# Fourteen block products for the output projection, and mixer A's gates moved behind its queries, keys and values

## The chip, the cores and the metric

The kernel runs on one core of one Trainium2 chip. A core has TensorE (matmuls, written to PSUM), VectorE, ScalarE, GpSimd, SyncE, whose queue issues most of the DMAs, and 16 DMA engines. In the profile they are PE (PEld for its weight loads), DVE, ACT, POOL and SP. The metric is the device time of one execution in microseconds.

## The reference

One encoder layer on 512 tokens of width 2048, with 16 meta tokens put in front (528 positions). All is float32.

```
hn   = rmsnorm(h, pre_norm_g)
proj = hn @ w_in                                  # 2048 -> 6656 columns
qa, ka, va, ga, qb, kb, vb, gb = split(proj)
ya = gqa_axial(qa, ka, va) * silu(ga)             # 8 heads of 128, 2 key/value heads, axial rotary
yb = diff_attn_alibi(qb, kb, vb) * silu(gb)       # 8 heads, each softmax1 - lam * softmax2, then a norm
y  = concat(ya, yb) @ w_out                       # 2048 x 2048
out = (h + rmsnorm(y, post_norm_g))[meta tokens dropped]
```

Mixer A norms queries and keys per head (RMS, times a gain), turns them by a rotary angle of the token's row and column, and attends. Mixer B subtracts two softmaxes with a distance penalty and norms the result per head.

## The kernel before

Every float32 product is done with three matmuls on float32r parts: an operand is split in a high part (`hi`, ScalarE, L325; for weights L158) and a low part (`lo`, VectorE, L328; for weights L159), and high x high, low x high and high x low are added in PSUM. So each dense column block of 128 over 16 slices of the inner dimension takes 48 matmuls of 512 columns (`REAL`), or 96 of 264 when the meta tokens are needed too (`KEYS`). All matmuls come from one line (`mm`, L63), all transposes from another (`transpose`, L66).

The order of TensorE is written by hand. `Lanes` (L45) has a planner's clock: each matmul adds its cost (512 columns 0.216 us by that clock, 264 columns 0.111), and each attention step is a generator that yields the lag after which its next step is due (the table `LAG`, L32). While a dense block runs, `lanes.poll()` after every three matmuls lets due steps in. `finish_head` runs a head's steps to their end at once (`force`), jumping the clock ahead to each due time, with no dense matmuls between. Everything so recorded stays in that order on TensorE (`keep_in_program_order`). The other engines' order is chosen by the framework's scheduler, apart from the loads through `load` (L143), which keep theirs too.

Weights come in chunks of 512 KB through `fetch`, which keeps two chunks ahead of the one in use; staging tiles, high parts and low parts have three buffers each. `wsplit` splits a chunk under a priority `rank[0]`.

Stages: loads of x and the first blocks; mixer B's heads (for each head a value, a key, a query and a gate block, with the attention of the head before beside them); mixer A's blocks in the order key 0, value 0, key 1, value 1, queries of group 0, two gates, queries of group 1, six gates (`GATES`); then the output. A head of mixer B has scores, softmax, a transposition of p through the PSUM tiles of the tag "tr" (two buffers), p times v, and `finish_B` with its norm matmul "ss" and the product with the gate. A head of mixer A multiplies p times v with its gate on VectorE (L585). Heads are written to DRAM (`oscr`).

The output (L827 on) takes 512 columns at a time. Groups 0 and 3 are computed whole (`dense_out`): 16 slices, 4 row tiles, 3 matmuls. The last four heads run beside group 0. Groups 1 and 2 are computed together from seven block products of 256 rows x 1024 inner x 512 columns (`product`), which need sums of blocks of w_out and sums of halves of the heads. The sums of weights are made in DRAM during mixer B, by a copy on SP's queue and an accumulating DMA on GpSimd's (`weigh`, 16 of each). At the end each row tile is scaled by its norm, added to the residual and written (`row_block`, L1028).

Of the kernel before, what the change touches and what calls it, by code (L numbers as in the profile page):

```python
# [10 lines left out]
F32 = mybir.dt.float32  # L11
# [24 lines left out]
LATE = ()  # L36
# [7 lines left out]
class Lanes:  # L44
# [13 lines left out]
    def mm(self, out, lhsT, rhs, start, stop):  # L58
# [4 lines left out]
        self._add(self.nc.tensor.matmul(out, lhsT, rhs, start=start, stop=stop), us)  # L63
# [45 lines left out]
def kernel(ctx: ExitStack, tc: tile.TileContext, xT, xn, xm, w_s, w_t, w_q, w_o,  # L109
# [8 lines left out]
    wp = ctx.enter_context(tc.tile_pool(name="wp", bufs=3))  # L118
    dr = ctx.enter_context(tc.tile_pool(name="dr", bufs=1, space=DRAM))
# [55 lines left out]
    for i in range(16):  # L175
# [3 lines left out]
    xh, xl = [[xp.tile([P, 576], F32R, name=f"x{n}{k}", tag=f"x{n}{k}")[:, :NT]  # L179
               for k in range(KT)] for n in "hl"]  # L180
# [77 lines left out]
    for t in (TT, 0, 1, 2, 3):  # L258
        rows = P if t < TT else NM
        src = xn[t * P:(t + 1) * P, :] if t < TT else xm  # L260
        for j in range(2 if t < 2 else 4):
# [4 lines left out]
            st = ap.tile([P, w], F32, name="xns", tag=tag, bufs=2 if t < 2 else 4)[:rows]  # L266
# [28 lines left out]
    cosT = ctile([P, TT, P], "cosT", src=cos_d, pool=ap)  # L295
    sinT = ctile([P, TT, P], "sinT", src=sin_d, pool=ap)
# [74 lines left out]
    def values(pss):  # L371
# [8 lines left out]
        def turn():  # L380
            tr = ptr.tile([P, 512], F32, name="tr", tag="tr")
# [5 lines left out]
            yield LAG["bank"]  # L387
            tr = ptr.tile([P, 512], F32, name="tr", tag="tr")
# [7 lines left out]
    def gate(pss, name):  # L396
        g = ap.tile([P, SEQ], F32, name=name, tag="g", bufs=4)
# [5 lines left out]
    pv_last, p_live = [None], [0]  # L403

# [14 lines left out]
    def p_times_v(pts, v, done, gate_of):  # L419
# [28 lines left out]
        while gate_of is not None and len(gA) <= gate_of:  # L448
            yield 0.3
        pv = ptr.tile([P, 512], F32, name="pv", tag="tr")  # L450
# [7 lines left out]
        mm(o, vm, pm, start=False, stop=True)  # L458
        done(o)
# [48 lines left out]
    def finish_B(h, o):  # L508
        while gB[h] is None and h not in LATE:
            yield 1.0  # L510
# [15 lines left out]
        if h in LATE:  # L526
            gB[h] = ap.tile([P, SEQ], F32, name=f"gB{h}", tag="g", bufs=4)
            nc.scalar.activation(gB[h], o, AF.Copy, scale=sgc)
        else:
            nc.vector.scalar_tensor_tensor(out=gB[h], in0=o, scalar=sgc, in1=gB[h],  # L530
                                           op0=ALU.mult, op1=ALU.mult)
# [171 lines left out]

# [429 lines left out]
```

## Time and profile before

| | us |
|---|---|
| median of 3 runs | 925.81 |
| lowest and highest | 925.52, 925.96 |
| the profiled execution | 925.19 |
| its span, first to last instruction | 923.4 |
| granted TensorE clock, share | 0.998 |

The span is what the trace covers; 1.8 us of the profiled execution lie around it. Busy times of engines overlap, so they don't add up to the span. Matmuls are pipelined and their ends are modelled: a matmul of 512 columns is shown as 0.39 us though the next one starts after about 0.23, so the pace is read from starts, or from a long unbroken stretch of the chain. A group "xN" has N instructions; the mean is of one of them.

### The profile page before, as it was taken

How to read it: one execution, taken by the hardware profiler on the slowest of the kernel's cores; microseconds unless marked ns; L12 is line 12 of the kernel's file. 1: busy time of each engine (PE TensorE's matmuls, PEld its weight loads, DVE VectorE, ACT ScalarE, POOL GpSimd, SP SyncE). 2: the span in 40 equal slices, each digit the busy share in tenths (PEclk: the TensorE clock that was granted, in tenths of full speed). 3: DMA queues.
4: the chain of work that ended last, by engine and by line, in shares of the span. 5: the costliest groups of instructions: out<-in, count | busy, mean ns of one | idle time of the engine just before them, and what ended most of it. 6: DMA issues, size and time to landing. Idle time of an engine off the chain costs nothing.

```text
span 923.4 us, 14263 instructions
## 1 busy us (share of the span) xinstructions
PE 911.5 (99%) x5498; PEld 807.2 (87%) x5498; DVE 576.7 (62%) x1029; ACT 486.5 (53%) x849; POOL 120.4 (13%) x164
## 2 busy tenths in 40 slices
PE   9999999999999999999999999999999999999995
PEld 8999898998989899898999888888888888888884
DVE  6676575847567575665766247447645574654797
ACT  6564564638455474654754254437555662524661
POOL 0102010111101010010010020115111111200110
PEclk9999999999999999999999999999999999999999
DMA  9845533644536364231223223221222162775884
GB/s 342 284 140 144 152 108 111 159 128 144 142 109 178 92 169 139 70 104 69 85 67 102 92 84 98 70 80 58 81 74 76 57 217 91 263 221 166 296 308 183
DMA packets 43892, 128.11 MB, mean 139 GB/s; under 512 B 5104, under 2 KB 9072, under 8 KB 43568
## 3 DMA queue, kind: packets, MB, share of 16 engines
q1 hardware_dynamic: 40416, 115.66, 37.1%
q0 software_dynamic: 3264, 11.54, 6.7%
q8 instruction: 43, 0.70, 0.3%
q14 instruction: 25, 0.20, 0.1%
q10 hardware_dynamic: 144, 0.01, 0.0%
HBM read 118.80 MB, written 25.17 MB: 156 GB/s over the span
## 4 chain that ended last, share of the span: by engine, by line
PE 93%; DVE 4%; ACT 1%; issue 1%; POOL 0%; DMA 0%; DVEq 0%; ACTq 0%; POOLq 0%
PE pd L63 60%; PE po L63 16%; PE sc L63 7%; PE pv L63 5%; PE tr L66 5%; DVE y L1028 1%; DVE wl L159 1%; PE ss L63 0%; DMA gcol<-in_gpre_dram 0%; DVE l L328 0%; DVE y L1040 0%; DVE qn L605 0%; POOL ssh L247 0%; DVE y L1034 0%; ACT jk L602 0%
## 5 line engine op out<-in xcount | busy, mean ns | idle before, releaser
L63 PE MATMUL pd<-xh,wh 128*128 128x264 f32 (+1 forms) x992 | 331.8, 334 | 0.2 <-ACT wh L158 0.2
L63 PE MATMUL pd<-xl,wh 128*128 128x264 f32 (+1 forms) x992 | 323.0, 326 | 0.0
L63 PE MATMUL pd<-xh,wl 128*128 128x264 f32 (+1 forms) x992 | 322.7, 325 | 0.1
L158 ACT ACTIVATE wh<-st 128x1024 fp32r<-128x1024 f32 (+2 forms) x147 | 152.8, 1040 | 210.3 <-issue 88.0
L159 DVE TENSOR_TENSOR wl<-st,wh 128x1024 fp32r<-128x1024 f32 (+2 forms) x147 | 176.4, 1201 | 113.7 <-ACT wh L158 112.6
L63 PEld LDWEIGHTS pd<-xh,wl 128*128 128x128 f32 x992 | 186.4, 188 | 16.3 <-DVE wl L159 0.3
L63 PEld LDWEIGHTS pd<-xh,wh 128*128 128x128 f32 x992 | 186.7, 188 | 11.7 <-ACT wh L158 0.4
L63 PEld LDWEIGHTS pd<-xl,wh 128*128 128x128 f32 x992 | 187.1, 189 | 10.6 <-DVE xl L187 0.4
L490 ACT ACTIVATE p<-p,mx 128x528 f32<-128x528 f32 x64 | 47.0, 734 | 43.2 <-DVE mx L482 42.9
L63 PE MATMUL po<-wh,oh 128*128 128x512 f32 x176 | 69.5, 398 | 0.1
L63 PE MATMUL po<-wh,ol 128*128 128x512 f32 x176 | 68.2, 390 | 0.2 <-DVE ol L328 0.2
L63 PE MATMUL po<-wl,oh 128*128 128x512 f32 x176 | 68.2, 390 | 0.0
L325 ACT ACTIVATE ph<-tr 128x512 fp32r<-128x512 f32 x64 | 37.5, 590 | 37.7 <-PE tr L66 37.4
L328 DVE TENSOR_TENSOR pl<-tr,ph 128x512 fp32r<-128x512 f32 x64 | 43.3, 687 | 15.5 <-ACT ph L325 15.1
L482 DVE CUSTOM_DVE_ANT_0 p<-sc,dist 128x528 f32<-128x528 f32 x64 | 44.8, 700 | 11.5 <-PE sc L63 11.1
L63 PE MATMUL pd<-wh,xh 128*128 128x512 f32 x128 | 51.6, 403 | 0.0
L66 PE MATMUL tr<-ident,p 128*128 128x128 f32 (+1 forms) x320 | 50.6, 272 | 0.1
L63 PE MATMUL pd<-wl,xh 128*128 128x512 f32 x128 | 50.1, 391 | 0.0
L63 PE MATMUL pd<-wh,xl 128*128 128x512 f32 x128 | 50.0, 391 | 0.0
L66 PEld LDWEIGHTS tr<-ident,p 128*128 128x128 f32 (+1 forms) x320 | 37.1, 131 | 11.2 <-DVE pl L328 1.0
L495 POOL TENSOR_SCALAR p<-p,sm 128x528 f32<-128x528 f32 x32 | 23.0, 718 | 170.8 <-DVE sm L492 157.6
L580 POOL TENSOR_SCALAR p<-p,smA 128x528 f32<-128x528 f32 x32 | 26.3, 820 | 142.5 <-DVE smA L579 109.9
(205 smaller groups left out, 1479.4 us busy)
## 6 DMA issues: line engine op xcount, KB each, us to landing
st<-in_w_t_dram SPq DMA_DIRECT2D x82, 512.0 KB, 3.8
st<-in_w_o_dram SPq DMA_DIRECT2D x24, 512.0 KB, 3.9
ws<-in_w_o_dram POOLq DMA_DIRECT2D x16, 512.0 KB, 5.8
st<-in_w_q_dram SPq DMA_DIRECT2D x16, 512.0 KB, 3.5
st<-ws SPq DMA_DIRECT2D x16, 512.0 KB, 4.3
xs<-in_xT_dram SPq DMA_DIRECT2D x16, 264.0 KB, 5.3
ws<-in_w_o_dram SPq DMA_DIRECT2D x8, 512.0 KB, 5.1
ws<-ws SPq DMA_DIRECT2D x8, 512.0 KB, 5.0
```

The lines of the kernel that those rows point to most:

```text
L63: self._add(self.nc.tensor.matmul(out, lhsT, rhs, start=start, stop=stop), us)
L66: self._add(self.nc.tensor.transpose(out, in_, ident), 0.109)
L158: splits.append((nc.scalar.activation(wh[:, c], st[:, c], AF.Copy), nc.vector.tensor_tensor(out=wl[:, c], in0=st[:, c], in1=wh[:, c].bitca ...
L159: nc.vector.tensor_tensor(out=wl[:, c], in0=st[:, c], in1=wh[:, c].bitcast(F32), op=ALU.subtract)))
L325: nc.scalar.activation(dst, src, AF.Copy)
L328: nc.vector.tensor_tensor(out=dst, in0=src, in1=h.bitcast(F32), op=ALU.subtract)
L482: nc.vector.tensor_tensor_reduce(out=two(p), in0=sc[:, :, :HALF], in1=two(dist[:, w0:w0 + NT]), scale=-0.125 / slope(h), scalar=3.0e38, op ...
L490: nc.scalar.activation(p2[m], p2[m], AF.Exp, scale=-1.0, bias=mx[:, m:m + 1], accum_out=sm[:, m:m + 1])
L495: nc.gpsimd.tensor_scalar(out=p2[0], in0=p2[0], scalar1=sm[:, 0:1], scalar2=1.0, op0=ALU.mult, op1=ALU.mult)
L580: nc.gpsimd.tensor_scalar(out=p, in0=p, scalar1=sm, scalar2=1.0, op0=ALU.mult, op1=ALU.mult)
L1028: order(nc.vector.scalar_tensor_tensor(out=v, in0=v, scalar=ry[t], in1=xres[t, g], op0=ALU.mult, op1=ALU.add))
```

## The change

- **Output.** Columns are paired (0 with 3, 1 with 2), and both pairs go through seven block products: fourteen instead of two whole groups and seven products. Sums of products are made in PSUM where they can be: the product of mixer B's first half is copied out and the bank then goes on accumulating mixer A's part, and likewise for others (`more=True`, no start flag). There are 32 sums of weights in DRAM instead of 16, so `weigh` is called with 2 at some places.
- **Mixer A.** The order of blocks is key 0, value 0, queries of group 0, queries of group 1, key 1, value 1, then all eight gates. The head's p times v is copied from PSUM by ScalarE to a tile `oA`, and `gate_A` multiplies it after its gate block. Each gate block ends with `finish_head` of its head. Mixer B's last head is finished after value 0; before, it was after key 1. The lag scA falls from 5.4 to 4.6. Steps of keys and values don't start while a p times v is open (`whole`). Rotary tables hold half as many columns, and `rope` has five operations instead of four.
- **Heads to the output.** Mixer B's halves are loaded into the tiles of y that are written late (y[i][3], y[i][0]), mixer A's heads into y[.][1] and y[.][2]; their high and low parts lie where x lay. Later half heads come through the gate's tiles, three sums for each of four pairs.
- **Tail.** Rows 2 and 3 are written during the thirteenth product, rows 0 and 1 during and after the fourteenth; the last tile's row blocks all come after its own gain.

The core of the diff (a line of "..." marks what is left out):

```diff
-           pB=8.0, ss=6.0, qA=2.35, scA=5.4, pA=4.14, rope=10.2, head=3.85, fin=1.35, qn=1.4, norm=4.0)
-GATES = [[0, 1], [2, 3, 4, 5, 6, 7]]
+           pB=8.0, ss=6.0, qA=2.35, scA=4.6, pA=4.14, rope=10.2, head=3.85, fin=1.35, qn=1.4, norm=4.0)
...
+    def gate_A(h, pss):
+        finish_head(NH + h)
+        g = gp.tile([P, SEQ], F32, name="gt", tag="gt")
         nc.vector.tensor_tensor(out=g, in0=pss[0], in1=rB[:, NM:], op=ALU.mult)
         nc.scalar.activation(g, g, AF.Silu)
+        nc.vector.tensor_tensor(out=oA[h], in0=oA[h], in1=g, op=ALU.mult)
+        nc.sync.dma_start(out=oscr[4 + h // 2][h % 2], in_=oA[h])
+        waiting[0] -= 1
...
-            last = spawn_pv(v_task, p_times_v(pts, v, lambda pv, half=half: nc.vector.tensor_tensor(
-                out=gs(half), in0=pv, in1=gs(half), op=ALU.mult), h), LAG["pA"])
+            last = spawn_pv(v_task, p_times_v(pts, v, lambda pv, half=half: nc.scalar.activation(
+                oA[h][:, half * 256:(half + 1) * 256], pv, AF.Copy), h), LAG["pA"])
...
-    kA, vA = [], []
-    for i in range(2):
-        pss = dense_T(KEYS)
-        finish_head(NH - 2 + i)
-        kA.append(keys_A(pss))
-        vA.append(values(dense_T(KEYS)))
...
-    for grp in range(2):
-        qn, q_task = queries_A(grp)
...
-        for h in GATES[grp]:
...
-            gA.append(gate(dense_T(REAL), f"gA{h}"))
+    pss = dense_T(KEYS)
+    finish_head(NH - 2)
+    kA = keys_A(pss)
+    vA = values(dense_T(KEYS))
+    finish_head(NH - 1)
     zed.append(ap.tile([P, DW], F16, name="zed", tag="dist", bufs=1))
     nc.vector.memset(zed[0], 0.0)
+    start_heads(0, *queries_A(0), kA, vA)
+    second_q = queries_A(1)
+    kA = keys_A(dense_T(KEYS))
+    start_heads(1, *second_q, kA, values(dense_T(KEYS)))
...
+    for h in range(NH):
+        gate_A(h, dense_T(REAL))
     lanes.finish_all()
     att.close()
-    rank[0] = 40
+    xst.close()
+    rank[0] = 0
...
+    for i in range(4):
+        for g, half in ((3, lo_), (0, hi_)):
+            st = y[i][g].rearrange("p (i q) -> p i q", i=2)
+            nc.sync.dma_start(out=st, in_=oscr[i].rearrange("i p q -> p i q")[:, :, half])
+            of_B.append(st)
+    for i in range(4):
+        st, sd = of_B[2 * i:2 * i + 2]
+        split(b0[i], st)
+        TTv(out=sd, in0=st, in1=sd, op=SUB)
+        split(t1[i], sd)
+    def bring_A(j):
+        st = y[j // 2][1 + j % 2]
+        nc.sync.dma_start(out=st, in_=oscr[4 + j // 2][j % 2])
+        hi(oh[j], st)
+        lo(ol[j], st, oh[j])
...
+    def first_half(p, pool, tasks):
+        r0, r1 = PAIRS[p]
+        pa = product(of_t(b0), banks(pool), beside=tasks[0])
+        rank[0] = 40
+        for u, ps in enumerate(pa):
+            nc.scalar.activation(y[u][r1], ps, AF.Copy)
+        pb = product(of_t(t1), banks(pool), beside=tasks[1])
+        for u, ps in enumerate(pb):
+            nc.scalar.activation(y[2 + u][r1], ps, AF.Copy)
+        product(of_a(0), pa, more=True, beside=tasks[2])
+        for u, ps in enumerate(pa):
+            square(u, r0, ps)
+            by_gain(u, r0, ps)
+        return product(of_a(1), pb, more=True, beside=tasks[3])
+    def second(p, pool, pb, beside):
+        r0, r1 = PAIRS[p]
+        pss = product(of_t(t2), banks(pool), beside=beside)
+        for u, ps in enumerate(pss):
+            TTv(out=y[u][r1], in0=ps, in1=y[u][r1], op=ADD)
+            TTv(out=y[2 + u][r0], in0=pb[u], in1=y[u][r1], op=ADD)
+            square(2 + u, r0, y[2 + u][r0])
+            by_gain(2 + u, r0)
+            TTv(out=y[2 + u][r1], in0=y[2 + u][r1], in1=y[u][r1], op=ADD)
+    for j in range(4):
+        bring_A(j)
+    two_by = every(2, lambda: next(sum_steps, None))
+    held = [first_half(0, pd2, (lambda i: bring_A(4 + i), None, two_by, two_by))]
...
+    held.append(first_half(1, pd, (two_by, two_by, sum_and_load, sum_and_load)))
+    second(0, pd2, held[0], lambda i: residual())
+    second(1, pd, held[1], lambda i: residual())
...
+    third = [product(of_t(t3), banks(pd2))]
+    for u, ps in enumerate(third[0]):
+        third_done(2 + u, ps)
+    third.append(product(of_t(t3), banks(pd)))
+    for u, ps in enumerate(third[1]):
+        last_block(2 + u, ps)
+    for t in (2, 3):
+        order(by_gain(t, 2))
+        turned(t)
+        for g in (0, 3, 1, 2):
+            row_block(t, g)
+    product(of_t(t4), third[0], more=True, ahead=4)
+    for u, ps in enumerate(third[0]):
+        third_done(u, ps)
     def end(u, ps):
         last_block(u, ps)
+        order(by_gain(u, 2))
+        turned(u)
+        for g in (0, 3, 1, 2):
+            row_block(u, g)
+    product(of_t(t4), third[1], more=True, done=end)
```

More of the change, by code (lines that the diff above doesn't have):

```diff
@@ new lines @@
+    sums = [[[dr.tile([P, 1024], F32, name=f"ws{p}{n}{i}", tag=f"ws{p}{n}{i}") for i in range(4)]
+             for n in range(4)] for p in range(2)]
+    steps, adds = [], []
+    for p in range(2):
+        S = sums[p]
+        steps += [(S[0][i], block(p, 1, 0, i), block(p, 1, 1, i)) for i in range(4)]
+        steps += [(S[1][i], S[0][i], block(p, 0, 0, i)) for i in range(4)]
+        steps += [(S[2][i], S[1][i], block(p, 0, 1, i)) for i in range(4)]
+        steps += [(S[3][i], block(p, 0, 0, i), block(p, 1, 0, i)) for i in range(4)]
@@ new lines, in weigh, with wlast @@
+    def weigh(n=1):
+        for _ in range(n):
+            if adds:
+                dst, src = adds.pop(0)
+                nc.gpsimd.dma_start(out=dst, in_=src, accum_op=ALU.add)
+            if steps:
+                dst, src, add = steps.pop(0)
+                load(dst, src)
+                adds.append((dst, add))
+    def wlast(i):
+        st = wp.tile([P, 1024], F32, name="st", tag="st")
+        nc.sync.dma_start(out=st, in_=block(1, 1, 1, i))
+        ws = []
+        for j in range(2):
+            wh, wl = [op.tile([P, 512], F32R, name=f"w{x}", tag=f"o{x}{2 * i + j}") for x in "hl"]
+            src = st[:, j * 512:(j + 1) * 512]
+            with tc.high_priority(rank[0]):
+                hi(wh, src)
+                lo(wl, src, wh)
+            ws.append((wh, wl))
+        return ws
@@ L868, with operand @@
-    for j in (0, 2):
-        bring(j)
-    first = dense_out(0, pd)
+    start_heads(0, *queries_A(0), kA, vA)
+    second_q = queries_A(1)
+    kA = keys_A(dense_T(KEYS))
+    start_heads(1, *second_q, kA, values(dense_T(KEYS)))
+    assert not steps and not adds
+    NP = TT // 2 * P
+    lo_, hi_ = slice(0, NP), slice(NP, SEQ)
+    TTv, SUB, ADD = nc.vector.tensor_tensor, ALU.subtract, ALU.add
+    def operand(tag, pools, i0=0, i1=4):
+        return [[pool.tile([P, 2, NP], F32R, name=f"{tag}{x}{i}", tag=f"{tag}{x}{i}")
+                 for x, pool in zip("hl", pools)] for i in range(i0, i1)]
@@ L880, in heads_of @@
-    def heads_of(i, half, dma):
-        t = yp.tile([P, 2, NP], F32, name="ts", tag="ts", bufs=6)
-        dma.dma_start(out=t, in_=oscr[i].rearrange("i p q -> p i q")[:, :, half])
-        return t
-    def operand(tag, i, src):
-        h, l = [yp.tile([P, 2, NP], F32R, name=f"{tag}{x}{i}", tag=f"{tag}{x}{i}") for x in "hl"]
-        hi(h, src)
-        lo(l, src, h)
-        return h, l
-    for i in range(4):
-        last[i] = yp.tile([P, 1024], F32, name=f"wx{i}", tag=f"wx{i}")
-    t1, t2, t3, t4 = [], [], [], []
@@ new lines, with fill @@
+    pad(op, "opad", 224)
+    t3 = operand("t3", (yp, yp), 0, 1)
+    yp.tile([P, 512], F32, name="jko", tag="jko")
+    pad(yp, "ypad", 384)
+    y = [[None] * 4 for _ in range(TT)]
+    def fill(places):
+        for t, g in places:
+            y[t][g] = ytile(t, g)
+    fill([(t, 3) for t in range(TT)])
+    gpB = yp.tile([P, DM], F32, name="gpB")
+    fill([(t, g) for t in range(3) for g in (1, 2)])
+    fill([(t, 0) for t in range(TT)])
+    pad(yp, "zpad", 128)
+    t3 += operand("t3", (yp, yp), 1)
@@ new lines, with half_of @@
+    for i in range(4):
[8 more added lines that the diff above has]
+        lo(ol[j], st, oh[j])
+    def half_of(i, half):
+        t = gp.tile([P, 2, NP], F32, name="ts", tag="g", bufs=4)
+        load(t, oscr[i].rearrange("i p q -> p i q")[:, :, half])
+        return t
@@ L936, in step, with banks, product @@
+    def banks(pool):
+        return [pool.tile([P, 512], F32, name="po", tag="pd") for _ in range(2)]
+    def product(ops, pss, more=False, beside=None, done=None, ahead=2):
         def step(u, i, ws):
```

358 lines of the change are left out of this document (120 added, 238 removed).

## The prediction

> **What bounds the kernel now.** I read the page first, for the engine that is never idle:
>
> ```profile
> span 923.4 us, 14263 instructions
> PE 911.5 (99%) x5498; PEld 807.2 (87%) x5498; DVE 576.7 (62%) x1029; ACT 486.5 (53%) x849; POOL 120.4 (13%) x164
> ...
> GB/s 342 284 140 144 152 108 111 159 128 144 142 109 178 92 169 139 70 104 69 85 67 102 92 84 98 70 80 58 81 74 76 57 217 91 263 221 166 296 308 183
> ...
> PE 93%; DVE 4%; ACT 1%; issue 1%; POOL 0%; DMA 0%; DVEq 0%; ACTq 0%; POOLq 0%
> ...
> L158 ACT ACTIVATE wh<-st 128x1024 fp32r<-128x1024 f32 (+2 forms) x147 | 152.8, 1040 | 210.3 <-issue 88.0
> L159 DVE TENSOR_TENSOR wl<-st,wh 128x1024 fp32r<-128x1024 f32 (+2 forms) x147 | 176.4, 1201 | 113.7 <-ACT wh L158 112.6
> ...
> L63 PE MATMUL po<-wh,oh 128*128 128x512 f32 x176 | 69.5, 398 | 0.1
> ...
> L325 ACT ACTIVATE ph<-tr 128x512 fp32r<-128x512 f32 x64 | 37.5, 590 | 37.7 <-PE tr L66 37.4
> L328 DVE TENSOR_TENSOR pl<-tr,ph 128x512 fp32r<-128x512 f32 x64 | 43.3, 687 | 15.5 <-ACT ph L325 15.1
> ...
> ts<-oscr SPq DMA_DIRECT2D x12, 256.0 KB, 4.3
> ```
>
> TensorE is busy for 911.5 of 923.4 us and is 93% of the chain that ended last. So the time is the number of matmuls by their pace, plus the few places where TensorE is not fed. The view by stretches, cut at the stages of the program, shows those places:
>
> ```profile
> 473.10:489.00 15.90, 15.83 (x131) 15.42 (x131) 8.78 (x16) 7.37 (x14) 0.40 (x1) 1.00 0.23 68
> ...
> 546.50:733.90 187.40, 186.88 (x1040) 158.99 (x1039) 111.41 (x233) 101.24 (x205) 41.24 (x55) 1.00 0.24 75
> 733.90:787.00 53.10, 52.78 (x293) 44.09 (x292) 30.83 (x54) 27.08 (x45) 11.09 (x15) 1.00 0.45 142
> 787.00:914.00 127.00, 127.00 (x561) 104.91 (x559) 89.61 (x118) 61.26 (x95) 11.54 (x14) 1.00 0.70 241
> 914.00:923.40 9.40, 0.10 (x1) 0.00 (x0) 5.96 (x10) 1.02 (x3) 0.00 (x0) 0.79 0.59 226
> ```
>
> The columns are us, TensorE busy with its matmuls, then weight loads, VectorE, ScalarE, GpSimd, granted clock, DMA share and GB/s. The third row is mixer A from the end of group 0's queries to the last gate, the fourth the first output group with the last heads beside it, the fifth the rest of the output, the last the tail. Nothing but the tail is visibly idle. The small waits that exist stand in the chain (us, duration, what) and in the list of waits:
>
> ```profile
> 734.68 1.28 ACT L399
> 735.98 0.63 ACT gA L399
> 736.61 0.53 ACT oh L325
> 737.16 0.70 DVE ol L328
> 737.91 0.73 PE po L63 x2
> ...
> 786.92 116.32 PE po L63 x513
> ```
>
> ```profile
> PE sc L63 <- DVE qlA L328: 0.4, 1, 0.4
> ```
>
> **What it removes.** Counts come from the code, a pace from the chain. Output before: two groups of 512 columns computed whole, 16 x 4 x 3 = 192 matmuls each, and two groups through seven block products of 4 x 2 x 2 x 3 = 48, 336 in all; together 720. The group view by forms has them as 176 of the row above, 32 of the row below and as many of its sister with v, each three times over (the two other terms of the split): 3 x 240 = 720.
>
> ```profile
> L63 PE MATMUL po<-wh,uh 128*128 128x512 f32 x32 | 12.4, 389 | 0.0
> ```
>
> After: both pairs of groups go through seven products, 14 x 48 = 672. 513 matmuls in 116.32 us are 0.2267 us each, so 48 fewer are **-10.9 us**. The products that now accumulate into a bank that was already copied out issue the same 48. No other matmul is added or removed.
>
> Two old waits go. Group 1's queries are now normed long before head 4 asks for them (keys and values lie between), so the wait on qlA goes. The wait at 737, where the first output matmuls stood behind a Silu with its table load (1.28 + 0.63) on ScalarE, loses its place. The stretches show 0.52 + 0.32 us of visible idle there; matmul ends are modelled and hide up to 0.17 us at each of some four stops. I take **-1.6 us** (-0.8 to -2.2).
>
> **What it adds: the last head of mixer B loses its cover.** Before, head 7 is forced to its end (finish_head) after three key/value column blocks of mixer A; after, already after two, because the second keys and values now come behind the queries. The first row by stretches is that third block. What runs in it, by forms, is 97 dense matmuls,
>
> ```profile
> L63 PE MATMUL pd<-xh,wh 128*128 128x264 f32 x32 | 9.7, 303 | 0.0
> ```
>
> (and its two sisters), and 34 others: ten transposes of p, five each of values and keys, thirteen of p times v, one or two of the norm. 97 x 0.12 = 11.6 of the 15.83 us are cover that goes elsewhere; 4.2 us remain, and they hang on each other through the two banks of the tag "tr". TensorE's order is the written one, so group 0's queries wait behind them. The chain: an eviction of p, the transpose of keys with its two evictions, then p times v and the norm:
>
> ```profile
> 476.31 0.67 DVE L328 TENSOR_TENSOR pl<-tr,ph 128x512 fp32r<-128x512 f32 x1
> ...
> 479.74 0.44 PE tr L66 x4
> 480.22 0.60 ACT L325 ACTIVATE kh<-tr 128x512 fp32r<-128x512 f32 x1 [0.38 <-PE tr L66]
> 480.85 0.69 DVE L328 TENSOR_TENSOR kl<-tr,kh 128x512 fp32r<-128x512 f32 x1 [0.56 <-ACT kh L325]
> ...
> 483.97 0.68 PE pv L63 x6
> 486.08 0.12 PE pv L63
> 486.24 0.39 ACT L502 ACTIVATE oB<-pv 128x256 f32<-128x256 f32 x1 [2.99 <-PE pv L63]
> 486.66 0.63 ACT L512 ACTIVATE sq<-oB 128x512 f32<-128x512 f32 x1
> 487.32 0.63 ACT L325 ACTIVATE sh<-sq 128x512 fp32r<-128x512 f32 x1
> 487.99 0.69 DVE L328 TENSOR_TENSOR sl<-sq,sh 128x512 fp32r<-128x512 f32 x1 [1.53 <-ACT sh L325]
> 489.08 0.46 PE ss L63 x2
> ```
>
> One turn of a bank is about 2.0 us (479.6 to 481.5); for the smaller tiles I estimate 1.3 to 1.6 from the same rows. The order by due times is p, p, values, p (32 rows), keys, value, key, p times v, norm. On one bank lie p, values, keys, last key: 2.6 (2.0, and 0.6 until ScalarE has done a weight split) + 2.0 + 2.0; on the other p, p32, value, p times v: first 3.3, then 1.6 and 1.6, so p times v starts some 6.6 to 7.4 us in; it takes 13 x 0.118 = 1.5 us; from its last matmul to the second norm matmul the rows give 2.8 us, then 0.23. Together 11.4 us, less the 4.2 of work that was there before: **+7.2 us**. The lower end is 6.0 (evictions never queue), the upper 9.0 (a weight split of 1.2 us gets ahead on VectorE, and one of 1.04 on ScalarE).
>
> **The way into the output.** The first product needs mixer B's halves, staged in output tiles that lie over dead attention tiles; by the order of allocation the first lies over the last p tiles. By the planner's due times the last transposes of p fall 2.3 us ahead of the last gate's end, and the last p times v (1.5 us) is forced just behind it. A staged half then needs 4.3 us to land (the row ts<-oscr), 0.6 for the high part, 0.7 for the low one, beside the last gate's Silu and table load on the same ScalarE, as at 734.68. High part ready 2.6 to 3.6 us after the gate, p times v done at 1.6; the second matmul waits 0.5 more for the low part: **+1.8 us** (0.3 to 4.0). If attention finished earlier, this would be near zero. On SP's queue a staged load that waits for its tile holds back the weight loads behind it; three chunks are buffered, 8.2 us of products, so that stays covered as long as the wait is under some 4 us.
>
> **The feed of the first two products.** VectorE has, by the rows L159 and L328: eight weight splits (9.6), four low parts of b0 (2.8), four differences and low parts of t1 (5.5), eight low parts of mixer A's heads (5.5) and the last gate (1.4): 24.8 us against 2 x 48 x 0.2267 = 21.8 of TensorE. Two splits lie ahead of the stage, and the heads' low parts may slip into the third product. I take **+1.0 us** (0 to 5).
>
> **The rest of the output** has 56 weight chunks of 512 KB in 152 us where before 44 were loaded; with 16 half heads, residuals, gains and output it moves about 45 MB, 296 GB/s. The slices at 296 and 308 in the GB/s row lie inside the unbroken 513 matmuls. VectorE by count: 67 us of splits, 30 of operands, 36 on y, 133 of 152. **+0.4 us** (0 to 2).
>
> **Tail.** The rows of VectorE after the last matmul:
>
> ```profile
> 914.54 0.68 DVE L1034 TENSOR_TENSOR y<-y,po 128x512 f32<-128x512 f32 x1
> ...
> 917.26 2.74 DVE L1028 SCALAR_TENSOR_TENSOR y<-y,ssy,xr 128x512 f32<-128x512 f32 x4
> ```
>
> Two row blocks and a gain stood between these; they now stand ahead, where VectorE still does tile 0's four blocks (2.74), so the last difference starts later by what the reciprocal gains: **+0.2** (-0.5 to +1.5).
>
> **Mixer A's pace.** scA falls by 0.8 at three places a head, up to 19 us over eight heads; the stage's cover falls by nearly as much (240 us from 546.5 to 787 before; 224 us of the same work from group 0's queries to the last gate after). The copy after p times v moves from VectorE to ScalarE, and rope has one more operation on VectorE; both engines are near 55 to 60% in the third row. **+0.3 us** (0 to 2). Mixer B's extra weight sums (32 DRAM copies and 32 accumulations instead of 16) fill GpSimd and DMA: GpSimd is busy for 13%, the GB/s row is at 60 to 180 there. Cost 0; an accumulation that waits for its copy could hold up p behind it on GpSimd, but there is slack: the eviction of p at 476.31 was done seven us ahead of its matmul at 483.97.
>
> **Sum.** -10.9 - 1.6 + 7.2 + 1.8 + 1.0 + 0.4 + 0.2 + 0.3 = **-1.6 us** against the profiled execution's own 925.19 us (span 923.4 and 1.8 around it), 923.6. That execution lies 0.6 under the median of 925.81, on which the same step gives **924.2**. A measurement of this kernel tells about 0.2% (1.85 us) from no change, so the forecast lies on that edge.
>
> **Rivals.** (1) *The clock falls.* While TensorE stands nearly idle behind head 7, the clock could drop. The trace has the slow clock at the start, before it had been busy, and in the tail, where the granted share averages 0.79 over 9.4 us, about 5.4 us at full and 4.0 at half:
>
> ```profile
> 1.21 3.70 PE L63 MATMUL hot<-heat 128*128 128x256 f32 x16 [1.21 <-DVE heat L173]
> ```
>
> Sixteen matmuls of 256 columns take 3.70 us there, 0.22 each against 0.118 in p times v: near half pace for 3.7 us. For it: 7 us with little more than 1 us of matmuls. Against it: no gap in it is as long as the tail's 5.4 us. It would slow p times v and the first queries, 1.7 to 3.9 us, I take 2.5: **926.7 us**. The Trainium skill, page "TensorE: Matmul & The Clock Gate", section "Part 1: The HAM clock gate", says that the clock falls to half after an idle window of about 3.4 us and returns after one as long that was busy; by that rule the price would be about 1.7 us. The tail's row agrees that idleness drops it; no run here shows how little work counts as idle.
>
> (2) *The new waits stay at their lower ends.* -12.5 + 6.0 + 0.5 = -6.0, **919.8 us**: evictions never queue and the staged halves come in time. For it speaks that VectorE and ScalarE have little else to do behind head 7; against it that every eviction there must be in its best place.
>
> (3) *The output's first products starve*, the case on the other side. Place: the first two products. It decides when the eight low parts of mixer A's heads go ahead of the weight splits (24.8 against 21.8 us), or when weights, both mixers' heads and the gains, some 10 MB in 24 us, meet the 342 GB/s that the first slice shows as the most moved: 29 us. Price 5 us and more: -1.6 + 5.0 = **929.2 us**. Against it: half of mixer B's tiles can be loaded early.
>
> (4) That the change doesn't do what it says can be excluded for the matmuls, which are counted in the code.
>
> **How the numbers follow.** Forecast 0.5, clock 0.2, lower ends 0.2, starving 0.1. The forecast's own range is 922.3 to 926.3, nearly half of it beyond the edge of faster; the clock case is mostly within 0.2%, a third slower; lower ends are faster; starving is slower. Faster 0.5 x 0.45 + 0.2 = 0.42, same 0.5 x 0.55 + 0.2 x 0.65 = 0.40, slower 0.18. The range reaches to 919.3 and to 929.2.
>
> **What would show it.** In the trace after: 672 output matmuls at 0.227; a stretch of about 11 us behind the second key/value pair of mixer A with some 4 us of matmuls, ended by the norm matmul ss; its granted clock; a stop of 1 to 3 us ahead of the first output matmul; no stop at head 4; products without a break. I am wrong if head 7's end costs under 5 us, or if the output's later products stop.

## The result and the profile after

The changed kernel takes **945.66 us** (median of 4 runs, 945.28 to 947.59), the kernel before 925.68 beside it (925.52 to 925.96): a ratio of 1.022, 95% interval 1.0202 to 1.0237. The profiled execution took 945.67 us with a span of 943.9, 20.5 more than the span before. The forecast was 924.2 with a range up to 929.2; the time lies 16.5 us above that range.

The page of the changed kernel first (busy time of each engine, then its shares of the chain that ended last):

```profile
PE 911.0 (97%) x5450; PEld 804.2 (85%) x5450; DVE 589.4 (62%) x1041; ACT 505.1 (54%) x877; POOL 121.5 (13%) x168
...
PE 86%; DVE 5%; ACT 4%; DMA 3%; issue 1%; POOL 1%; SPq 0%; DVEq 0%; ACTq 0%; POOLq 0%
```

TensorE has 48 instructions fewer. It was busy for 99% of the span before; now 33 us of the span are not covered by it, and it has fallen from 93% to 86% of the chain. The view by stretches of the changed kernel, cut at its stages, says where (from:to and length in us, TensorE busy, weight loads, VectorE, ScalarE, GpSimd, granted clock, DMA share, GB/s):

```profile
473.90:489.05 15.15, 7.77 (x38) 5.84 (x37) 7.87 (x17) 6.80 (x13) 0.40 (x1) 0.77 0.13 38
489.05:532.80 43.75, 43.75 (x187) 36.03 (x186) 13.32 (x13) 10.05 (x14) 0.00 (x0) 0.96 0.29 81
...
586.80:631.80 45.00, 40.90 (x325) 40.12 (x325) 34.98 (x88) 26.11 (x78) 17.36 (x23) 0.96 0.15 48
631.80:771.50 139.70, 136.54 (x785) 115.35 (x785) 68.98 (x129) 76.89 (x127) 18.09 (x29) 1.00 0.24 78
771.50:800.00 28.50, 22.79 (x87) 16.83 (x86) 21.32 (x28) 16.86 (x27) 0.00 (x0) 0.94 0.80 284
800.00:933.40 133.40, 133.40 (x589) 110.17 (x587) 98.75 (x121) 71.90 (x104) 8.16 (x8) 1.00 0.77 257
933.40:943.90 10.50, 0.05 (x1) 0.00 (x0) 6.53 (x11) 1.02 (x3) 0.00 (x0) 0.67 0.53 200
```

Four stretches lose. Behind value 0 of mixer A, up to the first queries, 15.15 us pass (row 1). Beside the second keys and values TensorE idles 4.10 us (row 3), beside the gates 3.16 (row 4). In the first two products 87 matmuls take 28.5 us, in which 28.5 / 0.2267 = 125.7 would have had room: 8.8 us lost (row 5). The rest of the output has no gap at all (row 6: 133.40 of 133.40, 0.226 a matmul). And the clock is under 1.00 in rows 1, 2, 3 and 5, where before it was under it only in the tail, of the stretches shown. A cut at the clock's own changes shows when:

```profile
476.16:479.57 3.41, 0.99 (x6) 0.53 (x6) 2.63 (x5) 0.74 (x3) 0.00 (x0) 1.00 0.30 56
479.57:486.40 6.83, 4.76 (x19) 3.86 (x19) 2.27 (x6) 1.48 (x6) 0.40 (x1) 0.50 0.12 49
486.40:489.81 3.41, 1.58 (x6) 1.09 (x7) 0.76 (x2) 3.31 (x5) 0.00 (x0) 1.00 0.00 0
489.81:493.22 3.41, 3.41 (x10) 2.64 (x9) 3.23 (x4) 0.14 (x1) 0.00 (x0) 0.50 0.00 0
595.63:599.04 3.41, 0.88 (x8) 0.66 (x6) 3.33 (x9) 1.57 (x5) 2.27 (x4) 1.00 0.00 0
...
790.19:793.60 3.41, 1.05 (x3) 0.59 (x4) 2.70 (x4) 2.50 (x4) 0.00 (x0) 1.00 0.49 199
```

A window of 3.41 us with little in it is followed by one or two at a clock of 0.50 (behind the last two rows, 599.04 to 602.45 and 793.60 to 797.01). Where dense matmuls fill the slow window, half of it is lost, 1.7 us.

The span's budget, from these rows and those of before:

| | us |
|---|---|
| 48 output matmuls less | -10.9 |
| behind mixer B's last head: 15.0 us for 4.2 of work, of which 1.6 by slow p times v; and 1.7 of slow clock in the queries | +12.5 |
| mixer A's stage: 4.10 + 3.16 idle, 1.7 of slow clock | +9.0 |
| the first two products | +8.8 |
| tail, 10.50 instead of 9.40 | +1.1 |
| start and mixer B (the same stretch ends at 445.1, before at 444.1) | +1.0 |
| what is left over, put down to the two old waits and not measured by itself | -1.0 |
| sum | +20.5 |

A stop, here and below, is counted from the start of one matmul to the start of the next, less their usual distance; the view of waits gives a little less for the same.

### The profile page after: what moved, and what is told of

The parts are those of the page before. It is cut to its first block, busy times and chain, and to the rows that moved or that the text cites. A ratio compares the mean times of both kernels' runs of the same rounds, so it can differ in the third digit from the quotient of the medians.

```text
span 943.9 us, 14282 instructions
## 1 busy us (share of the span) xinstructions
PE 911.0 (97%) x5450; PEld 804.2 (85%) x5450; DVE 589.4 (62%) x1041; ACT 505.1 (54%) x877; POOL 121.5 (13%) x168
## 4 chain that ended last, share of the span: by engine, by line
PE 86%; DVE 5%; ACT 4%; DMA 3%; issue 1%; POOL 1%; SPq 0%; DVEq 0%; ACTq 0%; POOLq 0%
PE pd L60 57%; PE po L60 13%; PE sc L60 6%; PE pv L60 5%; PE tr L63 4%; DVE wl L157 1%; DVE y L1041 1%; DMA gpB<-in_gpost_dram 1%; ACT wh L156 1%; DMA st<-ws 1%; DMA xs<-in_xT_dram 1%; DMA st<-in_w_o_dram 0%; POOL ssh L245 0%; ACT jk L616 0%; PE ss L60 0%
## 5 line engine op out<-in xcount | busy, mean ns | idle before, releaser
L156 ACT ACTIVATE wh<-st 128x1024 fp32r<-128x1024 f32 (+2 forms) x159 | 165.7, 1042 | 231.1 <-PE pd L60 98.9
L157 DVE TENSOR_TENSOR wl<-st,wh 128x1024 fp32r<-128x1024 f32 (+2 forms) x159 | 191.3, 1203 | 118.5 <-ACT wh L156 117.3
L512 DVE SCALAR_TENSOR_TENSOR p<-p,c 128x528 f32<-128x528 f32 x32 | 24.5, 766 | 31.0 <-POOL p L510 31.0
L741 POOL DMA_DIRECT2D ws<-in_w_o_dram x32 | 26.7, 835 | 120.1 <-DMA ws<-in_w_o_dram 66.1
L599 POOL TENSOR_SCALAR p<-p,smA 128x528 f32<-128x528 f32 x32 | 23.4, 733 | 145.2 <-DVE smA L598 129.0
L457 POOL TENSOR_SCALAR pm<-pm 32x256 fp32r<-32x256 f32 x32 | 21.2, 662 | 143.7 <-ACT pm L330 140.9
```

The source lines that it names most:

```text
L156: splits.append((nc.scalar.activation(wh[:, c], st[:, c], AF.Copy), nc.vector.tensor_tensor(out=wl[:, c], in0=st[:, c], in1=wh[:, c].bitca ...
L157: nc.vector.tensor_tensor(out=wl[:, c], in0=st[:, c], in1=wh[:, c].bitcast(F32), op=ALU.subtract)))
L512: nc.vector.scalar_tensor_tensor(out=p2[0], in0=p2[1], scalar=c2, in1=p2[0], op0=ALU.mult, op1=ALU.add)
L599: nc.gpsimd.tensor_scalar(out=p, in0=p, scalar1=sm, scalar2=1.0, op0=ALU.mult, op1=ALU.mult)
L741: nc.gpsimd.dma_start(out=dst, in_=src, accum_op=ALU.add)
```

## The experiments

**The last head behind the first queries.** One call is moved (lines are shortened by "..."):

```diff
-    finish_head(NH - 1)
-    zed.append(...)
-    start_heads(0, *queries_A(0), kA, vA)
+    first_q = queries_A(0)
+    finish_head(NH - 1)
+    zed.append(...)
+    start_heads(0, *first_q, kA, vA)
```

> Head 7 of mixer B is forced to its end behind the first queries of mixer A instead of ahead of them; nothing is left out. Theory (lost cover): the 15.15 us stretch behind the first values holds 4.2 us of work that has dense matmuls beside it now, so about 10.9 us go, and the two clock drops that follow it (in p times v and in the first queries, 1.6 and 1.7 us): 945.7 - 11 to - 14 = 932 to 935 us. Rival (only moved): mixer A's first heads come later by what the stop takes, since their scores wait for the last reader of the distances: 943 to 946 us.

Measured: 932.64 us, 13.0 less; ratio to the kernel before 1.0082 (1.0066 to 1.0098). Its stretch by time:

```profile
473.10:489.00 15.90, 15.67 (x86) 12.69 (x85) 8.15 (x16) 6.10 (x11) 1.18 (x1) 1.00 0.22 66
```

TensorE idles 0.23 us in the stretch, the clock is full, and no new stop appears later. So the loss was cover.

**The same move in the kernel before.** There `finish_head(NH - 1)` goes from behind key 1 to behind value 0:

```diff
-        finish_head(NH - 2 + i)
+        if i == 0:
+            finish_head(NH - 2)
         kA.append(keys_A(pss))
         vA.append(values(dense_T(KEYS)))
+        if i == 0:
+            finish_head(NH - 1)
```

> The kernel before, with one call moved: head 7 of mixer B is forced to its end behind the first values of mixer A, ahead of the second keys and values. Theory (lost cover): this alone makes the kernel before slower by 11 to 14 us: 937 to 940 us, with a stretch of some 15 us behind the first values that holds some 4 us of matmuls, and a granted clock of one half in the block after it. Rival (the stop comes from other parts of the change, such as the copy of p times v or the wider weight sums): under 930 us.

Measured: 939.04 us, 13.6 more than before; ratio 1.0152 (1.0134 to 1.017). The stretch behind value 0:

```profile
473.60:488.10 14.50, 7.52 (x30) 5.42 (x29) 6.91 (x14) 6.13 (x13) 0.40 (x1) 0.62 0.12 36
```

The same stop, with a clock of 0.62, appears in the kernel before, so no other part of the change is needed for it: two kernels, one call, the same 13 us with both signs.

**The clock by itself.** Matmuls that feed nothing, behind each forced step:

```diff
+    hot = pd.tile([P, 512], F32, name="hot", tag="pd")
...
             lanes.force()
+            for _ in range(4):
+                lanes._add(nc.tensor.matmul(hot[:, :256], ones_r, xh[0][:, :256], start=True,
+                                            stop=True), 0.0)
```

> The changed kernel, with four more matmuls of 128x256 (0.47 us in all) into an unused bank behind each step of the forced end of mixer B's head 7; they compute nothing that is used. Theory (waits and a slow clock that follows them): the waits stay, the clock does not fall at 479.6 and 489.8, which gives back 1.6 us in p times v and 1.7 us in the first queries, less some 0.5 us of matmuls in the way: 942 to 944 us. Rival (the dummies stand in the way of the chain, or the clock has other causes): 946 us or more.

Measured: 941.68 us, 4.0 less; ratio 1.0171 (1.0155 to 1.0187). Its stretches:

```profile
473.90:489.50 15.60, 11.79 (x88) 10.47 (x87) 7.92 (x17) 7.95 (x14) 0.40 (x1) 1.00 0.12 35
489.50:532.80 43.30, 43.30 (x192) 35.82 (x192) 13.20 (x13) 10.89 (x20) 0.46 (x2) 1.00 0.31 92
```

The gain is a little more than expected, its place only in part as expected. The forced stretch is hardly shorter (14.9 us instead of 15.0), as the dummies take most of the time that the faster p times v gives. The clock drops near 600 and 794 were gone too in this execution, though stops stood ahead of them still (2.6 us on qlA, 1.9 us on wh). Counted from the start of a matmul to the start of the same one in both traces, the 3.9 us less of the span are 0.2 up to the queries, 1.6 in the queries, 1.0 from there to the first output matmul and 1.8 in the output, less 0.7 that the tail took more. So the price of a stop has two parts: its own length, and up to 1.7 us more if the clock falls.

**The order of loads ahead of the output.**

```diff
-    nc.sync.dma_start(out=gpB, in_=gpost)
...
-    for j in range(4):
-        bring_A(j)
+    def gains_too(i):
+        two_by(i)
+        if i == 0:
+            nc.sync.dma_start(out=gpB, in_=gpost)
+
-    held = [first_half(0, pd2, (lambda i: bring_A(4 + i), None, two_by, two_by))]
+    held = [first_half(0, pd2, (bring_A, lambda i: bring_A(4 + i), gains_too, two_by))]
```

> The changed kernel; mixer A's first four heads are brought beside the first product and the last four beside the second, and the 1 MB of gains is loaded beside the third, instead of all ahead of the first. Theory (order on SP's queue): the weight chunk that lands at 790.89 lands some 6 us sooner, the stop of 2.96 us in the second product and the slow clock at 793.6 to 797 (1.7 us) go: 945.7 - 4 to - 6 = 940 to 942 us. Rival (VectorE and ScalarE are the bound there, 24.8 us of splits in 21.8 us): under 2 us, 944 to 946 us.

Measured: 940.76 us, 4.9 less; ratio 1.017 (1.0154 to 1.0186). In the changed kernel SP's queue reads (start, us, issue):

```profile
773.09 0.33 SPq L560 DMA_DIRECT2D oscr<-oA  x1
773.52 3.12 SPq L890 DMA_DIRECT2D y<-oscr  x6
776.74 0.41 SPq L922 DMA_DIRECT2D gpB<-in_gpost_dram  x1
777.19 4.20 SPq L901 DMA_DIRECT2D y<-oscr  x7
```

and the chain of the changed kernel goes on from there with a weight chunk, issued at 784.43, behind the seven loads:

```profile
784.43 6.46 DMA st<-ws
```

The weight chunk that the second product needs stands behind 1 MB of gains and seven heads, none of which is needed before the third product. With those later, the stop of 2.8 us on wh is gone, and the first two products take 24.8 us instead of 29.9, from the first matmul's start to the start of the first one behind them.

**Both edits together.**

> Both edits measured before in one kernel: head 7 of mixer B forced to its end behind the first queries (13.0 us alone), mixer A's heads brought beside the first two products and the gains beside the third (4.9 us alone). Theory (the two costs lie in different stages and add up): 945.66 - 13.0 - 4.9 = 927.8 us, 926.5 to 929. Rival (the second stop appears in another place once the first is gone, or the halves shared the same slow clock): 930 us or more.

Measured: 928.92 us; ratio 1.0039 (1.0025 to 1.0053). Inside the range, 1.1 us over the sum: the two losses are separate, and add.

**The last head's write off SP's queue.** The first row of that queue above waits for the last gate's product, with six staged loads behind it.

```diff
-        nc.sync.dma_start(out=oscr[4 + h // 2][h % 2], in_=oA[h])
+        (nc.gpsimd if h == NH - 1 else nc.sync).dma_start(out=oscr[4 + h // 2][h % 2], in_=oA[h])
```

> The two edits, and the last head's write to its scratch goes out on GpSimd's queue instead of SP's. Theory (that write, which waits for the last gate's product at 770.9 in the run with later loads, holds back six staged loads that were ready): the stops of 0.82 and 0.50 us in the first product go, perhaps more: 1 to 2 us under the two edits alone. Rival (the staged loads wait for their tiles' last readers, not for the queue): the same time within 0.5 us.

Measured: 926.93 us, 2.0 less than the two edits; ratio 1.0013 (1.0002 to 1.0024). The two stops in the first product went, as expected; the first two products take 22.6 us, counted as above. With 4.9 this makes 6.9 of the 8.8 us; what remains are stops of 1.16 and 0.68 at the first two output matmuls.

**Mixer A's stage: norms in steps.** Between the sums of squares and the gains now lie 4 us of the planner's time for the second queries (1.5 for the first) and 2 to 3 for keys (their lines are left out here):

```diff
         rstd(ss[:rows, :n], ss[:rows, :n], P, rows)
+        yield lag
         for i in range(n):
...
-                head_norm(qn, 4, gqB)
+                yield from head_norm(qn, 4, gqB, P, (1.5, 4.0)[g])
...
-                yield LAG["norm"]
+                yield (2.5, 8.0)[g]
```

> The two edits, and the norms of the second queries and of both keys are handed out in steps: the gains come some 2 to 4 us of TensorE's work behind the sums of squares (1.5 for the first queries, as long in all as before), the next tile of the second queries 8 us later. Theory (the norms stand in VectorE's row and wait there for GpSimd, ahead of the heads' low parts): the stops of 2.76 us at 583 and of 0.9 us at 608 and 611 in the run with the queries as cover go: 3 to 5 us under the two edits alone, with the slow clock that follows them (1.7). Rival (VectorE and ScalarE have too much work for these heads anyway): the stops move and the time is the same within 1 us.

Measured: 927.21 us, 1.7 less than the two edits without the last write's; ratio 1.0021 (1.0009 to 1.0032). That lies between the two texts, and the intervals of the two kernels overlap. Its stretches from 620 us on:

```profile
620.00:752.00 132.00, 131.86 (x759) 112.17 (x759) 70.32 (x131) 72.05 (x122) 17.88 (x28) 1.00 0.24 78
752.00:785.00 33.00, 27.80 (x113) 22.12 (x113) 23.58 (x32) 20.23 (x32) 1.18 (x1) 0.90 0.79 268
```

TensorE's idle time beside the gates fell from 3.16 us (the run of both edits) to 0.14, beside the keys (575 to 620) only from 4.48 to 3.55. But the heads ended later, so the last p times v and the staged halves behind it stood uncovered: 5.2 us idle around the start of the output and a slow clock (second row).

**The pace of mixer A's scores.** `scA` is 5.4 again, with the two edits.

> The two edits, and the lag between two scores of a head of mixer A is 5.4 us again, as in the kernel before. Theory (density: heads packed closer make the stops of mixer A's stage, 4 us up to the last keys and 3 us beside the gates): these fall to the half or less, while the last heads lose up to 19 us of cover, of which the tail of the attention behind the last gate shows some: stops of 3 to 5 us less, a stretch behind the last gate of 5 to 10 us more. Rival (the stops come from single events in the rows of VectorE and ScalarE, not from the pace): the stops stay at their sizes, and the time is longer by what is not covered at the end.

Measured: 928.54 us, no difference to the two edits (928.92); ratio 1.0037 (1.0024 to 1.005). Neither text has it whole. Idle time beside the gates fell from 3.16 to 1.07 us, beside the keys only from 4.48 to 3.80, and the stretch ahead of the output got the same gap as in the run above, in both a wait of 4.1 us on the high part of the first staged half. The pace makes some of the stops; a slower one moves them to the end.

**One of the two, with TensorE's order kept.** Both runs are the kernel with the two edits and the last write on GpSimd's queue, and one thing left out each:

```diff
         for t, qn in enumerate(res):
-            head_norm(qn, 4, gqB)
-            rope(qn, ...)
+            if g == 0:
+                head_norm(qn, 4, gqB)
+                rope(qn, ...)
```

> The kernel with the queries as cover, the later loads and the last write on GpSimd's queue, without the norm and the rotation of the second four heads' queries (they are left out; the order on TensorE stays as it was). Theory (the norms stand ahead of the heads' operands in the rows of VectorE and ScalarE): TensorE idles 4.46 us at 575 to 620 with them; without, the stop of 2.76 us at 583.5 goes and the idle time there falls to 2 us or less, the stops at 658, 681 and 696 stay: 926.9 - 2.5 to - 4.5 = 922.4 to 924.4 us. Rival (the heads' own pace makes the stops): the stop at 583 stays above 1.5 us and the time within 1 us of 926.9.

Measured: 923.3 us, 3.6 less; ratio 0.9968 (0.9951 to 0.9984).

```diff
-        nc.scalar.activation(g, g, AF.Silu)
+        nc.scalar.activation(g, g, AF.Copy)
```

> The same kernel, with a plain copy in place of the Silu of mixer A's eight gates (their Silu is left out, so ScalarE need not change tables between it and the exponentials). Theory (the stops of 1.26, 0.72 and 1.33 us at 658, 681 and 696 come from a gate's Silu with its table load ahead of qh or ph on ScalarE): all three go, the first product's stop of 1.16 us shrinks too, the stop at 583 stays: 926.9 - 3 to - 4.5 = 922.4 to 924 us. Rival (the stops come from VectorE's row or from the banks): they stay, and the time is within 1 us of 926.9.

Measured: 922.97 us, 4.0 less; ratio 0.9965 (0.9952 to 0.9978). By the ratios to the kernel before, which ran beside each, the two gains are 4.2 and 4.4 us. The waits of TensorE from 500 to 800 us, in the kernel with both:

```profile
PE tr L63 <- DVE qlA L333: 3.2, 2, 2.6
PE tr L63 <- DVE pl L333: 1.5, 2, 1.2
PE sc L60 <- ACT qh L330: 1.1, 1, 1.1
PE po L60 <- ACT ah L330: 1.0, 1, 1.0
...
```

without the second norm:

```profile
PE tr L63 <- DVE pl L333: 1.2, 1, 1.2
...
PE tr L63 <- DVE qlA L333: 0.6, 1, 0.6
...
```

and without the Silu, all that was left:

```profile
PE tr L63 <- DVE qlA L333: 2.6, 1, 2.6
PE po L60 <- ACT ah L330: 1.0, 1, 1.0
PE tr L63 <- ACT oA L604: 0.8, 1, 0.8
PE sc L60 <- DVE qlA L333: 0.7, 1, 0.7
PE po L60 <- DVE al L333: 0.4, 1, 0.4
```

Each takes away its own waits and leaves the other's: the norm the 2.6 us on qlA, the Silu those on pl and qh. One miss: the first product's stop (1.0 on ah) does not shrink without the Silu. The plain copy in its place takes the same 0.63 us there, and the last gate had no table load in the kernel with both either. How an earlier gate holds up TensorE stands in ScalarE's row by time, in the kernel with both:

```profile
655.51 1.28 ACT L558 ACT_TABLE_LOAD   x1 [0.45 <-DVE gt L557]
656.80 0.63 ACT L558 ACTIVATE gt<-gt 128x512 f32<-128x512 f32 x1
657.45 1.28 ACT L597 ACT_TABLE_LOAD   x1
...
659.48 0.58 ACT L330 ACTIVATE qh<-tr 128x512 fp32r<-128x512 f32 x1
```

Two table loads and the Silu are 3.2 us. The transposes for qh are done at about 656.7, so qh waits some 2.8 us behind them and an exponential in the same row. The Trainium skill, page "ScalarE: Activation LUTs", section "What ACT_TABLE_LOAD costs", gives a load about 1283 ns and about 1380 ns of drain besides. The first agrees with the 1.28; of the second no gap is seen between load and Silu here.

**Three kernels towards a faster one.** The kernel with the last write moved, plus the norms in steps and `scA` 4.3, so that the heads end sooner again:

> The queries as cover, the later loads, the last write on GpSimd's queue, the norms in steps, and the lag between scores of mixer A 4.3 us instead of 4.6, so that the heads end some 7 us sooner. Theory (the stops beside the second keys come from the norms' place in the rows, those at 658, 681 and 695 from where a gate's Silu falls, and the stop of 4.29 us ahead of the output from heads that end late): 926.9 - 3 to - 6 = 921 to 924 us, with a stop of at most 1.5 us ahead of the output. Rival (a closer pace brings back as much as it takes away): 926 to 929 us.

Measured: 924.05 us; ratio 0.9986 (0.9977 to 0.9995), at the slow edge of what was expected. No long stop ahead of the output any more, but a new wait of 3.6 us on pl near 622, with a slow clock behind it. (In the run with all edits below, which has the same wait, both norms stand in VectorE's row there.)

In the tail the last tile's difference goes ahead of two row blocks (without the norms in steps):

```diff
         last_block(u, ps)
+        if u:
+            for g in (1, 2):
+                row_block(0, g)
         order(by_gain(u, 2))
         turned(u)
-        for g in (0, 3, 1, 2):
+        for g in (0, 3, 1, 2)[:4 if u else 2]:
             row_block(u, g)
```

> The queries as cover, the later loads, the last write on GpSimd's queue, and in the tail the last difference of the output goes ahead of two of the four row blocks that stood before it on VectorE, with those two between it and its gain. Theory (VectorE's row sets the tail: the last difference starts 2.5 us behind its last matmul): 1.0 to 1.4 us less than without it, 925.5 to 926, the span behind the last matmul 9.7 to 10.1 us instead of 11.1. Rival (the writes on SP's queue, 0.9 us each, set the tail): the same time within 0.3 us.

Measured: 926.21 us, 0.7 less; ratio 1.0004 (0.9995 to 1.0012). The intervals overlap, so the 0.7 is not clear of noise. From the last matmul's start to the end it takes 10.6 us instead of 11.1: half of what was expected. In the other traces of these runs the same span varies from 10.65 to 11.53 us without this edit, and from 10.07 to 10.59 in the three with it. What holds the rest stays open.

All together:

> All of these edits together. Theory (they add up): 920 to 923 us, faster than the kernel before. Rival: the edits give back to one another what they take: 925 to 927 us.

Measured: **922.72 us**, ratio 0.9973 (0.9965 to 0.9982): 0.3% faster than the kernel before, a small gain but clear of its interval.

**The second norm sooner**, over before the keys' norm begins: the steps are `(1.5, 2.0)[g]` and `(2.5, 3.5)[g]`.

> All the edits, with the second queries' norms handed out in steps of 2.0 and 3.5 us instead of 4.0 and 8.0, so that they should be over before the second keys' norm begins. Theory (in the run with all edits both norms stand in VectorE's row at 612 to 624 and hold back a score's evaluation, by it an exponential and the high and low parts of p, until the transpose of values at 622.5 waits 3.77 us): this stop falls under 1 us and the slow clock behind it goes: 3 to 5 us less than 922.7, 917.5 to 920. Rival (the stop comes from where the heads' steps fall, which any shift may move): a stop of 2 us or more in another place of the stage and 921 to 925 us.

Measured: **922.51 us**; ratio 0.9968 (0.9956 to 0.998), the same as the run before. The stop at 622 is gone, and others came: on copies to oA, 2.2 us the longest. The rival has it: in this stage a shift of steps moves the stops. The first products of this kernel, from 0.6 us behind the first output matmul on:

```profile
757.00:785.00 28.00, 27.69 (x122) 22.92 (x123) 22.43 (x29) 18.78 (x28) 0.63 (x1) 1.00 0.94 334
```

TensorE is busy for 27.69 of 28 us at 334 GB/s, and VectorE for 22.4 us where the changed kernel has 21.3 in row 5 of its stretches. So what stopped the changed kernel there, at 284 GB/s, was neither bytes nor the amount of VectorE's work, but order.

**The stage's edits alone**: the changed kernel with these steps and `scA` 4.3, nothing else.

> The changed kernel with the norms in these steps and the lag between scores at 4.3 us, and nothing else: head 7 of mixer B forced ahead of the queries, the loads as changed. Theory (mixer A's stage loses some 9 us by the norms' place in the rows and by the pace, apart from the other two losses): 945.66 - 5 to - 8 = 937.5 to 940.5 us, the losses behind head 7 and ahead of the output as before. Rival (the stage's loss follows from the other two): 944 us or more.

Measured: 942.26 us, 3.4 less; ratio 1.0175 (1.0161 to 1.0189). The stage's loss is one of its own; these edits get back 3.4 of its 9.0 us, less than expected. In the traces 2.8 us of it lie between the queries and the first output matmul.

## Why the prediction was wrong

**The gain was right.** -10.9 us for 48 matmuls: there are 48 fewer, and the output is unbroken from 800 us on at 0.226 a matmul. The rest of the output, for which 0.4 was added, has no gap. For the two old waits, -1.6, the budget leaves -1.0, which no row measures.

**"The last head of mixer B loses its cover", +7.2, was mis-sized: 12.5.** The mechanism and the place (behind value 0; "behind the second key/value pair" is a slip) were as forecast. The step that failed is "p times v starts some 6.6 to 7.4 us in". In the chain of the changed kernel it starts 9.0 us in, counted from 474.07, the start of the transposes of p:

```profile
475.08 0.61 DVE kn L634
475.69 0.68 DVE vf L324 x2
476.37 1.13 DVE wl L157
477.50 0.61 DVE pl L333
...
479.48 0.70 DVE vl L333
...
480.23 1.13 PE tr L63 x4
...
482.01 0.70 DVE kl L333
...
483.07 3.16 PE pv L60 x13
```

The low part of p stands in VectorE's row behind a weight split, as in the upper bound, and behind the key's rotation and the value's halves as well: the first turn of the bank takes 4.1 us where the forecast had 2.6. The values' turn takes 2.1 (2.0 forecast), that of the keys 2.5 (2.0), since its transposes already run at the slow clock, and the last key 0.3 more. Without the slow p times v and queries the loss is 9.2 (15.0 less 1.6 of slow clock less 4.2 of work), about the forecast's upper bound of 9.0. The other 3.3 are the clock, which the forecast had only as a rival at 2.5 us and a chance of 0.2: p times v took 3.16 us for the 1.5 forecast, and the queries lost 1.7.

**"Mixer A's pace", +0.3 (0 to 2), was the step that failed altogether: 9.0.** Its argument was that two engines at 55 to 60% have room. Another section ("What it removes") counted the second queries' norm as a gain, since it is done long before head 4 asks, and did not ask where its instructions go: 16 sums of squares on ScalarE, four norms and four rotations on VectorE, ahead of the operands of heads that now run beside them. The chain of the changed kernel into the longest of these stops:

```profile
590.10 2.17 POOL pm L457
...
594.62 1.06 POOL ssh L245
...
595.71 0.81 DVE qn L619
...
597.81 0.67 DVE qn L633 x2
598.48 0.61 DVE qlA L333
```

GpSimd is late with ssh, the norm's gains (L619) wait for it in VectorE's row, and qlA waits behind the gains and the rotation. Without that norm 3.6 us are gone, without the gates' Silu 4.0. Both kinds of work were there before too, and their amount alone is not the cause: in the kernel before, the 45 us from 620 on have VectorE busy for 33.4 us and GpSimd for 16.4, and TensorE idles 0.52; in the changed kernel the 45 us of row 3 have 35.0 and 17.4, and TensorE idles 4.10. The pace is part of it (the run with 5.4 has less idle time), the rest is which step falls behind which; the runs settle the two sources, not a single place to mend.

**"The way into the output", +1.8, had the right size for another reason.** In the run with the queries as cover the first two output matmuls stop for 1.16 and 0.68 us, 1.84 together. The forecast let the first staged half land last. In the changed kernel the first two halves are issued from 766.08 on, and such loads land 3.1 to 4.3 us later there; but the high part starts only at 772.14. In ScalarE's row it stands straight behind the copy of the last p times v (771.86), and the last matmul of that starts at 771.54. The hit in the number is luck to that extent. The old wait at 737, which by the forecast "loses its place", has in this stop a successor of about its size.

**"The feed of the first two products", +1.0 (0 to 5), was mis-sized: about 7.** The forecast counted VectorE's work (24.8 us against 21.8) and bytes. It had seen the queue ("On SP's queue a staged load that waits for its tile holds back the weight loads behind it"), and took it as covered under some 4 us; the last write, the heads and the gains held the chunk back from 773.09 to 784.43. So the case on the other side, "The output's first products starve", came true by another condition than the one it was given. Bytes were no limit at the 342 GB/s that it took as the most moved: from 785.00 to 790.20 us the changed kernel moves 406.

**The tail, +0.2 (-0.5 to +1.5): +1.1**, in its range. **Mixer B, 0**: its stretch took 404.7 us after 404.6, with twice the sums of weights.

Of the causes, lost cover was in the forecast, the clock and the late feed were rivals at 0.2 and 0.1, and mixer A's rows were not seen. The rivals were priced as alternatives; they came together, and on top of it. Even with every term at its own upper bound the sum would have been 937.6 us.

## What to carry to other kernels

When a block of dense work is moved, list every engine's row at the place where it was and at the place where it goes: the cost is in what now stands ahead of an operand, not in the engine's share. Price a stop on TensorE at its length, and add half a clock window (1.7 us here) for the case that the clock falls; ask of each load in a queue whether it is needed sooner than the load behind it. A norm or a table change that nobody waits for still delays what is queued behind it.

## What the runs showed of the hardware

**A stop of one length costs 1.7 us more or not.** In two kernels the same stop of 2.76 us stands near 583 us. In the run with the queries as cover (columns as in the views by stretches above):

```profile
582.18:585.59 3.41, 1.46 (x13) 1.25 (x11) 3.04 (x9) 1.54 (x5) 2.82 (x4) 1.00 0.00 0
585.59:589.00 3.41, 2.76 (x13) 2.76 (x14) 3.41 (x8) 2.06 (x5) 1.17 (x1) 0.50 0.00 0
```

and in the run with both edits, cut at whole windows of 3.413 us back from the drop in its tail:

```profile
582.04:585.45 3.41, 1.75 (x15) 1.54 (x13) 3.04 (x10) 1.54 (x6) 3.12 (x4) 1.00 0.00 0
585.45:588.86 3.41, 2.46 (x21) 2.46 (x22) 3.41 (x9) 2.25 (x5) 1.17 (x1) 1.00 0.00 0
```

With 1.46 us of matmuls in its window the clock falls in the next, with 1.75 it doesn't. In the changed kernel 0.88, 0.99, 1.05 and 1.58 of 3.41 were few enough, and in the run with the last write moved the same stop left 1.49 in a window and the clock stayed at 1.00. So a window need not be empty, and where the stop lies against the windows matters; matmul ends are modelled, and no sharp bound between 1.46 and 1.75 comes out of these rows. The changes of the clock in the changed kernel are whole multiples of 3.413 us apart (599.04 to 793.60 is 57 of them). The Trainium skill, page "TensorE: Matmul & The Clock Gate", section "Part 1: The HAM clock gate", has such a window of 3413 ns that runs freely, and these rows agree.

**One operation of GpSimd takes 0.4 or 2.2 us.** The copy of 32 x 256 at 590.10 took 2.17 us in the chain above, beside a busy VectorE. In the run with the norms in steps one of the same shape took 0.40:

```profile
590.41 0.40 POOL L457 TENSOR_SCALAR pm<-pm 32x256 fp32r<-32x256 f32 x1
```

There VectorE is idle from 590.04 to 591.80 us. That VectorE's accesses stretch it fits these two rows, but in the run with all edits one took 0.55 us beside a busy VectorE, and no run tried it by itself: the cause stays open.
